# Inputs and outputs stored in memory in the order the chip uses them

## The chip, the core and the metric

The kernel runs on one core of a Trainium2 chip. The metric is the time of one execution in device microseconds (us); lower is better. Engines are TensorE (PE in the profile), VectorE (DVE), ScalarE (ACT), GpSimd (POOL) and SyncE (SP), which here issues the DMAs. Each takes its instructions in program order, and they wait for one another by semaphores.

## What is computed

One inference step of a two-layer decoder trunk on two groups that share the weights: a prompt of 512 tokens and 8 samples of 4 tokens, in float32. Layer 0 is an RWKV-7 time mixing with 32 heads of 64, layer 1 a gated MLP with causal spatial mixing in chunks of 128; each adds to a residual of width 1024, and a final RMS norm follows. What matters of layer 0:

```
def step(S, inp):                  # S: one state [value, key] per head
    r_t, w_t, k_t, v_t, kk_t, a_t = inp
    sa = einsum('bhvk,bhk->bhv', S, -kk_t)
    S = S * w_t + sa (kk_t * a_t)^T + v_t k_t^T
    return S, einsum('bhvk,bhk->bhv', S, r_t)
```

The step runs over the tokens; the prompt starts from a zero state, each sample from a state given as input (`state_wkv`, [value, key] per head). Outputs are the final states of both groups, the last projected row of each sequence (the token shift), the two groups' result rows, and the normalised v rows of the samples.

## The kernel before, in words

**Weights.** Every projection multiplies in three passes (high x high, high x low, low x high halves of float32 numbers), with 128 output features at a time. `load` (L110) brings a block of weights from memory as 8 pieces of 128 x 128, row by row out of the full matrix, on the SP queue; ScalarE makes the high half, VectorE the low half. The activations stand as [feature, token] with 272 columns per half (256 prompt tokens, 16 sample tokens).

**Start.** x is loaded with a token per partition, normalised and turned by TensorE transposes into the halves `hh` and `hl`. The parameter vectors come as rows (`r0`, `r1`, `r2`, `sst`) and are turned into columns `ng`, `prm1`, `prm2` and `ss` by transposes (L176, L225, L226, L231).

**Layer 0.** Sixteen pairs of heads p are worked on one after the other, each in many stages. Every stage is a Python generator whose `yield`s cut it into steps, and a table `AT` gives each step a due time in units (one unit is one set of three projection matmuls; a pair's four projections k, r, v, z are 64 units). `on(p, stage, ...)` puts step n of pair p at 64p + AT[stage][n], all steps are sorted by that time into `agenda`, and `play` issues them in this order. Inside `manual_schedule` this is the order of the instructions on PE, DVE, ACT, POOL and SP alike. A stage that takes 200 units is therefore spread over the periods of the next pairs. Pairs 14 and 15 have tables of their own (`smp14`, `gram15`, ...); the others share one. The stages that the steps of the prediction touch:

- `gram` (L574 on): TensorE multiplies keys with queries per chunk of 64 tokens (L584), VectorE masks the products (L587), and they go to memory and back in another layout: four stores to `du` (L592, in two steps of two at 56.2993 and 56.8544) and one load `lu` (L595, at 60.3741).
- `lanes`: inverts small triangular matrices on VectorE, beginning with `lu` times `ln` (L686, at 62.564); its result goes by `dz` through memory into `Zf` (L725, L729).
- `merge`: VectorE transposes blocks of `Zf` (L740), TensorE multiplies (L750, L751), and so on.
- `chain`: seven sequential state updates, a matmul `sb` (L890) and a VectorE update `RS` (L892) in turn; at the end TensorE transposes the final state (L900), ScalarE copies it, and it is stored.
- `sample`: four DMAs load a pair's sample states `sn` (L930) at 7.88, four transposes turn them (L934, at 64.4533), ScalarE copies them to `s0`; the steps of four tokens are solved by matrix products; VectorE adds the update to `s0` (L992) and multiplies by the decay (L994, at 119.608); four transposes turn the result back (L998, at 128.593), ScalarE copies it, and four DMAs store it (L1006) at 179.324.
- `tail` (L1061): VectorE makes the gated output `of`, stored to memory as `od` (L1063) at 179.55.
- `flip` (L799 on): in nine of the periods a block of x is loaded, turned by transposes (L813, L815) and stored to a scratch tensor `xfd`, from where the residual is loaded later.

**Layer 1** uses Tile's own order, not the table. The spatial weights are turned by transposes (L1337) and masked; u, v and z are projected; the shift outputs are turned at L1450.

## Time and profile before

| | |
|---|---|
| timed runs | 1279.21, 1276.22, 1279.21 us; median 1279.21 |
| profiled execution, first to last instruction (span) | 1272.1 us |
| runs above that span | 4.1 to 7.1 us |
| mean granted TensorE clock | 0.997 of full speed |
| moved by DMA | 124.34 MB in 271752 packets, 114673 of them under 512 B |
| share of the 16 DMA engines' time, main queue | 35.0% |

The page gives no time of the profiled execution beyond its span. In the rows, PE is TensorE multiplying, PEld its weight loads, and SPq, ACTq and so on an engine's issuing side. A row of a timeline is start, length, engine, source line, operation and tensors (out<-in), with the shapes and the count of merged instructions; a bracket at its end is idle time of the engine before it and what ended it. A row of the list of groups has the count, then the busy time in us and the mean length of one in ns. Lengths of matmuls overlap, so what one costs its engine is read from start to start.

### The profile page before, as it was taken

How to read it: one execution, taken by the hardware profiler on the slowest of the kernel's cores; microseconds unless marked ns; L12 is line 12 of the kernel's file. 1: busy time of each engine (PE TensorE's matmuls, PEld its weight loads, DVE VectorE, ACT ScalarE, POOL GpSimd, SP SyncE). 2: the span in 40 equal slices, each digit the busy share in tenths (PEclk: the TensorE clock that was granted, in tenths of full speed). 3: DMA queues.
4: the chain of work that ended last, by engine and by line, in shares of the span. 5: the costliest groups of instructions: out<-in, count | busy, mean ns of one | idle time of the engine just before them, and what ended most of it. 6: DMA issues, size and time to landing. Idle time of an engine off the chain costs nothing.

```text
span 1272.1 us, 36601 instructions
## 1 busy us (share of the span) xinstructions
PE 1244.5 (98%) x15279; PEld 1192.4 (94%) x15279; DVE 953.0 (75%) x2210; ACT 692.3 (54%) x1613; POOL 137.0 (11%) x346
## 2 busy tenths in 40 slices
PE   6999999999999999999999999999999999999997
PEld 5899999999999999999989899999999999999997
DVE  5789998989899898989988866472338656656466
ACT  5677567667766865776766562244343223223333
POOL 2212021111202111110211100110000000000000
PEclk9999999999999999999999999999999999999999
DMA  5422433432343344334333364422323232231511
GB/s 161 116 72 74 111 97 91 111 105 75 94 122 91 87 111 101 89 94 102 85 79 81 101 200 117 143 92 76 100 72 99 64 109 79 70 110 55 166 37 72
DMA packets 271752, 124.34 MB, mean 98 GB/s; under 512 B 114673, under 2 KB 264451, under 8 KB 271587
## 3 DMA queue, kind: packets, MB, share of 16 engines
q1 hardware_dynamic: 271587, 122.00, 35.0%
q8 instruction: 120, 1.97, 0.7%
q14 instruction: 45, 0.37, 0.1%
HBM read 102.02 MB, written 19.95 MB: 96 GB/s over the span
## 4 chain that ended last, share of the span: by engine, by line
PE 87%; DVE 5%; DMA 3%; ACT 2%; issue 1%; POOL 1%; SPq 1%; POOLq 0%; DVEq 0%; ACTq 0%
PE r_p L253 3%; PE v_p L253 3%; PE gz_p L253 3%; PE gu_p L253 3%; PE gz_p L255 3%; PE gz_p L254 3%; PE gu_p L255 3%; PE gu_p L254 3%; PE gv_p L1410 2%; PE k_p L253 2%; PE gv_p L1412 2%; PE gv_p L1411 2%; PE r_p L255 2%; PE r_p L254 2%; PE pgo L584 2%; PE v_p L254 2%
## 5 line engine op out<-in xcount | busy, mean ns | idle before, releaser
L253 PE MATMUL v_p<-hh,v_h 128*128 128x272 f32 x256 | 78.9, 308 | 0.9 <-ACT raw L396 0.9
L253 PE MATMUL r_p<-hh,r_h 128*128 128x272 f32 x256 | 78.5, 306 | 0.0
L253 PE MATMUL k_p<-hh,k_h 128*128 128x272 f32 x256 | 78.3, 306 | 0.0
L253 PE MATMUL z_p<-hh,z_h 128*128 128x272 f32 x256 | 77.8, 304 | 0.0
L253 PE MATMUL gz_p<-hh,gz_h 128*128 128x272 f32 x256 | 75.2, 294 | 0.0
L253 PE MATMUL gu_p<-hh,gu_h 128*128 128x272 f32 x256 | 74.2, 290 | 0.0
L255 PE MATMUL r_p<-hh,r_l 128*128 128x272 f32 x256 | 74.1, 289 | 0.0
L255 PE MATMUL gz_p<-hh,gz_l 128*128 128x272 f32 x256 | 74.0, 289 | 0.0
L255 PE MATMUL gu_p<-hh,gu_l 128*128 128x272 f32 x256 | 73.9, 289 | 0.0
L255 PE MATMUL z_p<-hh,z_l 128*128 128x272 f32 x256 | 73.8, 288 | 0.0
L255 PE MATMUL v_p<-hh,v_l 128*128 128x272 f32 x256 | 73.8, 288 | 0.0
L254 PE MATMUL gz_p<-hl,gz_h 128*128 128x272 f32 x256 | 73.8, 288 | 0.0
L254 PE MATMUL gu_p<-hl,gu_h 128*128 128x272 f32 x256 | 73.8, 288 | 0.0
L254 PE MATMUL v_p<-hl,v_h 128*128 128x272 f32 x256 | 73.7, 288 | 0.0
L254 PE MATMUL r_p<-hl,r_h 128*128 128x272 f32 x256 | 73.7, 288 | 0.0
L254 PE MATMUL z_p<-hl,z_h 128*128 128x272 f32 x256 | 73.7, 288 | 0.0
L255 PE MATMUL k_p<-hh,k_l 128*128 128x272 f32 x256 | 73.6, 288 | 0.0
L254 PE MATMUL k_p<-hl,k_h 128*128 128x272 f32 x256 | 73.6, 287 | 0.0
L1410 PE MATMUL gv_p<-gv_h,hh 128*128 128x256 f32 x256 | 73.3, 286 | 0.0
L1411 PE MATMUL gv_p<-gv_h,hl 128*128 128x256 f32 x256 | 72.1, 282 | 0.0
L1412 PE MATMUL gv_p<-gv_l,hh 128*128 128x256 f32 x256 | 72.0, 281 | 0.0
L255 PE MATMUL go__p<-goh,go_l 128*128 128x272 f32 x192 | 55.6, 289 | 0.0
(446 smaller groups left out, 4624.9 us busy)
## 6 DMA issues: line engine op xcount, KB each, us to landing
k_r<-rw_in SPq DMA_DIRECT2D x16, 512.0 KB
r_r<-rw_in SPq DMA_DIRECT2D x16, 512.0 KB
v_r<-rw_in SPq DMA_DIRECT2D x16, 512.0 KB
z_r<-rw_in SPq DMA_DIRECT2D x16, 512.0 KB
gu_r<-gm_in SPq DMA_DIRECT2D x16, 512.0 KB
gz_r<-gm_in SPq DMA_DIRECT2D x16, 512.0 KB
go_r<-gm_out SPq DMA_DIRECT2D x24, 256.0 KB
od<-of SPq DMA_DIRECT2D x16, 272.0 KB
```

Source lines behind the costliest of these rows:

```text
L253: T.matmul(ps, whi, ahi, start=first, stop=False)
L254: T.matmul(ps, whi, alo, start=False, stop=False)
L255: T.matmul(ps, wlo, ahi, start=False, stop=last)
L584: T.matmul(pg[h][:, 128 * j : 128 * j + 128], BK[rs, c].rearrange("p a b -> p (a b)"), AR[rs, :, c, :], start=True, stop=True)
L1410: T.matmul(o, ah, hi, start=k == 0 and i % 2 == 0, stop=False, skip_group_check=True)
L1411: T.matmul(o, al, hi, start=False, stop=False, skip_group_check=True)
L1412: T.matmul(o, ah, lo, start=False, stop=k == KD - 1, skip_group_check=True)
```

## The change

The host now hands over all inputs in the order in which the chip wants them and takes the outputs in the chip's order.

- Weight blocks: each partition's 8 x 128 numbers are contiguous (rows of 4 KB instead of 512 B). Sizes and engines of the loads stay.
- `ng`, `prm1`, `prm2` and `ss` are columns of the constants; 13 small loads, 11 transposes and 4 copies at the start go. The constants load is split at column 144 instead of 128 and its second part is longer.
- Sample states lie key by value: one load straight to `s0` (two buffers instead of one) and one store straight from it; 8 transposes, 2 ScalarE copies and 6 DMAs per pair go. The store's step is due at 120.608, one unit behind the decay multiply at 119.608 (pair 14: 111.185 after 110.185; pair 15: 154.2 after 153.2).
- The prompt's final state is stored as it is, in the step that also begins the y matmuls (134.984); its transpose and copy go. Before, the store was due at 189.592.
- `flip` and `xfd` go; the residual is loaded from an input `x_t`.
- The LoRA weights of a pair come by one load instead of two; the spatial weights come turned, and one multiply masks all eight; the shift output is stored as it stands.

The rest of the table `AT` is unchanged. The core of the diff:

```
         def load(name, src, nk, w=128, q=Q):
-            q.dma_start(raw[:, 0:nk, :], src.rearrange("(k p) f -> p k f", p=128))
+            q.dma_start(raw[:, 0:nk, :], src)
...
-            Q.dma_start(cst[:, 128:], A["consts"][:, 128:])
+            Q.dma_start(cst[:, 144:], A["consts"][:, 144:])
...
             py = [bank("py", t) for t in "sy"]
-            pf = bank("pfs", "g")
+            Q.dma_start(O["prompt_s"][p], SS[:, NCH, :])
...
-            T.transpose(pf[0:64, 0:128], SS[:, NCH, :], ident)
...
-            for bp in range(2):
-                for h in range(2):
-                    Q.dma_start(sn[64 * bp : 64 * bp + 64, :, 64 * h : 64 * h + 64], swk[bp, 2 * p + h])
-            yield
-            ps = bk("ps0", p)
-            for j in range(4):
-                T.transpose(ps[:, 128 * j : 128 * j + 128], sn[:, j, :], ident)
-            yield
-            s0 = l0.tile([128, 512], F32, name=f"s0{p}", tag="s0", bufs=1)
-            S.activation(s0, ps, AF.Copy)
+            s0 = l0.tile([128, 512], F32, name=f"s0{p}", tag="s0", bufs=2)
+            Q.dma_start(s0, A["state_s"][p])
...
             V.tensor_tensor(out=v8(s0), in0=v8(s0), in1=z["D"][:, 8:16, None].to_broadcast([128, 8, 64]), op=ALU.mult)
             yield
-            ps = bk("pso", p)
-            for j in range(4):
-                T.transpose(ps[:, 128 * j : 128 * j + 128], s0[:, 128 * j : 128 * j + 128], ident)
-            yield
-            so = l0.tile([128, 4, 128], F32, name=f"so{p}", tag="sn", bufs=2)
-            S.activation(so, c128(ps), AF.Copy)
-            yield
-            owk = O["sample_wkv"][0].rearrange("(j a) h v k -> a h v j k", a=2)
-            for bp in range(2):
-                for h in range(2):
-                    Q.dma_start(owk[bp, 2 * p + h], so[64 * bp : 64 * bp + 64, :, 64 * h : 64 * h + 64])
+            Q.dma_start(O["sample_s"][p], s0)
...
-            smp=(7.87945, 64.4533, 66.8469, 70.2306, ..., 115.687, 119.608, 128.593, 128.593, 179.324),
+            smp=(7.87945, 70.2306, ..., 115.687, 119.608, 120.608),
-            chain=(103.348, ..., 134.984, 135.175, 135.175, 136.551, 189.592),
+            chain=(103.348, ..., 134.984, 135.175, 135.175),
-            flip=(129.64, 132.271, 132.271, 141.972),
...
-            Q.dma_start(xT[:, m : m + 2], xfd[:, m : m + 2])
+            Q.dma_start(xT[:, m : m + 2], A["x_t"][:, m : m + 2])
...
-            for q in range(2):
-                wsr = lt.tile([128, 4, 128], F32, name=f"wsr{q}", tag="gz", bufs=3)
-                Q.dma_start(wsr, A["gm_ws"][0, 4 * q : 4 * q + 4].rearrange("g t s -> t g s"))
-                ps = wa("pws")
-                for j in range(4):
-                    T.transpose(ps[:, 128 * j : 128 * j + 128], wsr[:, j, :], ident)
+            Q.dma_start(wst, A["g_ws"])
```

## The prediction, made before the changed kernel was run

> **What bounds the kernel now.** I read the page first: engine shares, then the chain that ended last.

> ```profile
> PE 1244.5 (98%) x15279; PEld 1192.4 (94%) x15279; DVE 953.0 (75%) x2210; ACT 692.3 (54%) x1613; POOL 137.0 (11%) x346
> PE 87%; DVE 5%; DMA 3%; ACT 2%; issue 1%; POOL 1%; SPq 1%; POOLq 0%; DVEq 0%; ACTq 0%
> ```

> TensorE is busy 98% of the span and holds 87% of the chain. So each matmul that goes should bring the end nearer, as long as TensorE stays the engine that ends last. By stage (the table by stretches; its columns are PE, PEld, DVE, ACT, POOL busy with counts, granted clock, DMA share, GB/s):

> ```profile
> 300.00:400.00 100.00, 99.97 (x1512) 94.53 (x1513) 89.90 (x223) 70.15 (x181) 16.68 (x49) 1.00 0.37 96
> 950.00:1050.00 100.00, 100.00 (x859) 99.77 (x858) 68.03 (x141) 31.40 (x54) 1.43 (x2) 1.00 0.31 88
> ```

> In the gMLP stage (second row) VectorE has 32% to spare. In the RWKV stage (first row) it is at 90% beside a TensorE at 100%: two in-order queues, each feeding the other, almost equally full. What the change does to their meeting points decides, so I walked one turn of the 64-unit period (44.1 us), from the timeline of VectorE, then of TensorE:

> ```profile
> 355.98 0.24 DVE L1061 SCALAR_TENSOR_TENSOR of<-X,lnh,zs 128x32 f32<-128x32 f32 x1
> 362.53 0.68 DVE L994 TENSOR_TENSOR s<-s,D 128x512 f32<-128x512 f32 x1
> 365.05 0.41 DVE L686 TENSOR_TENSOR lu<-lu,ln 64x256 f32<-64x256 f32 x1
> 366.24 0.28 DVE L892 SCALAR_TENSOR_TENSOR RS<-sb,D,ND 128x64 f32<-128x64 f32 x1
> 395.03 0.69 DVE L587 TENSOR_TENSOR GK<-pge,cst 128x512 f32<-128x512 f32 x1 [0.61 <-PE pge L584]
> 406.64 0.68 DVE L994 TENSOR_TENSOR s<-s,D 128x512 f32<-128x512 f32 x1
> ```

> ```profile
> 365.87 0.33 PE L890 MATMUL sb<-RS,MB 128*128 128x64 f32 x2
> 366.03 0.61 PE L934 MATMUL ps<-cst,sn 128*128 128x128 f32 x4
> 366.48 0.60 PE L998 MATMUL pso<-cst,s 128*128 128x128 f32 x4
> 366.92 0.33 PE L890 MATMUL sb<-RS,MB 128*128 128x64 f32 x2
> 384.55 0.27 PE L750 MATMUL pm<-T,GK 64*64 64x64 f32 x1
> 393.82 0.37 PE L584 MATMUL pgo<-AR,BK 64*128 64x128 f32 x1
> ```

> These rows close a ring of true dependences. L994 (the sample state times its decay) ends at 363.21. VectorE reaches L686, the first operation of `lanes`, 1.84 later. L892 behind it ends 1.47 after L686 starts, and feeds the second sb matmul, 0.40 later. TensorE then runs densely to L750 (17.63) and on to the gram matmuls (9.27); VectorE masks them from 1.21 later and is dense until the next L994 ends at 407.32 (12.29). Sum 1.84 + 1.47 + 0.40 + 17.63 + 9.27 + 1.21 + 12.29 = 44.11, the period. The slack in the ring is small: about 0.25 before the sb matmul.

> The third queue is SP. Its timeline at that place:

> ```profile
> 356.25 0.34 SPq L1063 DMA_DIRECT2D od<-of  x1
> 356.64 3.77 SPq L592 DMA_DIRECT2D du<-GK  x4
> 362.10 0.59 SPq L595 DMA_DIRECT2D lu<-du  x1
> 400.75 2.57 SPq L592 DMA_DIRECT2D du<-GK  x4
> 404.90 0.59 SPq L595 DMA_DIRECT2D lu<-du  x1
> ```

> SP issues in program order and stands still at a DMA whose data are not ready: `od` goes out 0.03 after L1061 ends, and `du` only behind it. The four `du` stores and the load `lu` bring the gram products to `lanes`; L686 cannot start before `lu` lands.

> **The change, part by part.**

> *Transposes off TensorE.* Four of them take 0.45 (366.03 to 366.48) and 0.44 (366.48 to 366.92): 0.11 each from start to start, though each shows 0.27 long.

> ```profile
> L934 PE MATMUL ps<-cst,sn 128*128 128x128 f32 x64 | 9.7, 274 | 0.0
> L998 PE MATMUL pso<-cst,s 128*128 128x128 f32 x64 | 9.6, 273 | 0.0
> L813 PE MATMUL pxt<-cst,xr 128*128 128x128 f32 x32 | 4.8, 272 | 0.0
> L900 PE MATMUL pfs<-cst,RS 128*64 128x128 f32 x16 | 4.8, 298 | 0.0
> L1337 PE MATMUL pws<-cst,wsr 128*128 128x128 f32 x8 | 1.2, 275 | 0.0
> L1450 PE MATMUL psh<-cst,shl 128*128 128x128 f32 x4 | 0.7, 286 | 0.0
> ```

> These 188, with 8 small ones in the last flip and 11 at the start, at 0.11 each make 22.8 us. [...]

> *A new wait on SP.* Before, the sample state's store came after its transposes and copy, at 64p + 179.3, long after its data. Now it is at 64p + 120.608, one unit behind L994. In period p that is the store of p-1, at 64p + 56.608: between the first pair of `du` stores (56.2993) and the second (56.8544), with `lu` at 60.3741 behind. The second pair was issued around 358.5 to 360.4 while L994 ends at 363.21. So SP now stops for L994, and `du`, `lu` and L686 with it. After L994 ends: 0.03 to issue and 0.39 for the store (as `od`, 356.25 to 356.64), 1.28 for two `du` (half of 2.57), 1.58 until `lu` is issued (403.32 to 404.90), then its landing. For that:

> ```profile
> 539.15 0.59 SPq L595 DMA_DIRECT2D lu<-du  x1
> 541.73 0.41 DVE L686 TENSOR_TENSOR lu<-lu,ln 64x256 f32<-64x256 f32 x1
> 56.48 0.59 SPq L595 DMA_DIRECT2D lu<-du  x1
> 60.74 0.42 DVE L686 TENSOR_TENSOR lu<-lu,ln 64x256 f32<-64x256 f32 x1 [1.72 <-DMA lu<-du]
> ```

> In the first pair L686 found it landed 2.58 after issue; in the second it waited until 4.26. I take 2.58, the value of the steady stage. L994 to L686 becomes 0.03 + 0.39 + 1.28 + 1.58 + 2.58 = 5.86 instead of 1.84 (bounds 5.5, if `lu` lands as fast as a `du` store, 0.64 + 1.58, to 7.5).

> *The ring after.* 5.86 + 1.47 + 0.15 (an estimate of the 0.40 without its slack) + 17.08 (17.63 less four pxt, 0.44, and one pfs, 0.11) + 9.27 + 1.21 + 12.29 = 47.33: 3.22 more per period. The ps and pso transposes, the largest part removed, stood between the two sb matmuls, where TensorE now waits anyway: they give nothing there. It applies to lanes 1 to 13: with the schedules of 14 and 15, `lu` (55.849 and 39.979) is ahead of the store. 13 x 3.22 = 41.9.

> *Outside the ring.* One ps of stage 0, and ps and pso around stages 14 and 15: 6 x 0.36 = 2.2; three pfs 0.3; pws 0.9; psh 0.4; at the start 0.8. Together -4.6. The wait that opens the kernel:

> ```profile
> PE png L176 <- DMA r<-norm_g: 7.4, 1, 7.4
> PE pth L213 <- DVE xsh L204: 3.3, 1, 3.3
> ```

> png goes, but xsh, which ends that second wait, hangs on other work; no gain beyond the 0.16 of a copy.

> *The clock.* TensorE's hole before the second sb is 47.3 less some 42.9 of work: 4.4 us, in one piece, each period. What a hole does (stretches, columns as above):

> ```profile
> 19.00:21.00 2.00, 2.00 (x10) 1.61 (x10) 1.58 (x5) 2.00 (x6) 0.00 (x0) 0.52 0.18 51
> 21.00:23.00 2.00, 2.00 (x10) 1.50 (x10) 0.81 (x3) 0.63 (x2) 0.00 (x0) 0.63 0.48 134
> 1266.00:1268.00 2.00, 0.00 (x0) 0.00 (x0) 1.34 (x6) 1.57 (x4) 0.55 (x1) 1.00 0.38 158
> 1268.00:1270.00 2.00, 0.00 (x0) 0.00 (x0) 0.30 (x2) 0.28 (x1) 0.00 (x0) 0.59 0.91 375
> ```

> ```profile
> 1265.36 0.28 PE L1595 MATMUL pgl<-hh,gol 128*128 128x256 f32 x1
> ```

> After the last matmul (ends 1265.64) the clock fell at about 1268.36 (0.59 over two us): 2.7 us of idling were enough. At the start the means 0.52 and 0.63 say half clock for 96% and 74% of two stretches of 2 us, 3.4 us together, which costs 1.7 us of dense work. I take it that 8 of 10 holes cost that: 13 x 0.8 x 1.7 = 17.7 (bounds 0 and 13 x 2.5 = 32).

> *Priced at nothing.* Weight loads in rows of 4 KB: no matmul is released by one in the list of waits after the start; the next block's load is issued while the current one multiplies. Copies on ScalarE: 54% busy. The prompt-state store, now on SP ahead of the s0 and v loads, waits for the last L892; the v load slips behind it, and the plan uses that weight 11 units after its load (8.43 and 19.34). The longer constants load, the residual from memory, the one-piece mask of the spatial weights: each within 1 us either way.

> Sum: 41.9 - 4.6 + 17.7 = +55.0 on a span of 1272.1, about 1327. The runs' median lies 7.1 above the profiled span, kept: 1279.2 + 55.0 = 1334.

> **The rivals.**

> *Faster: TensorE's queue alone decides.* If SP passes the store without holding back `lu`, or VectorE has other work to absorb it, the 22.8 come off: 1256. For it: no wait over 0.3 on TensorE between 100 and 600. Against: the ring, each link of which is a queue order or data. The change turns faster where L994-to-L686 stays under 3.0 us: the period is then 0.35 longer, and 13 x 0.35 is the 4.6 saved outside the ring. 8%; the transposes' gain and a shrunken stall cancel (1279) in 4%.

> *The clock stays up.* The stall as above, but the holes don't lower the clock: 1279.2 + 41.9 - 4.6 = 1317. For it: the kernel before has no hole of this length in its middle, so no row shows one; the two falls above are at the start and at the end. 14%.

> *The clock falls only where a hole holds a whole 3.4 us stretch.* The clock at the start changed after 3.4 us; if it is set once per such a stretch, and only an entirely idle one lowers it, a hole of 4.4 us holds one in (4.4 - 3.4) / 3.4 = 3 of 10 periods: 1316.5 + 13 x 0.3 x 1.7 = 1323. Against: the fall 2.7 us after the last matmul, when no whole stretch had been idle. 12%. [...]

> *Change not effective* (the copies remain) can't be: the code that issues them is gone.

> **How the numbers follow.** Stall and clock 62% (1334), stall alone 14%, stall and some clock 12%, cancelled 4%, faster 8%. The slow cases' bounds: 13 x 0.36 = 5 under 1317 is 1312, less 5 for the edits priced at nothing, 1307; above, 13 x 1.64 = 21 over 1334 is 1355, and 1358 with a little more lost to the clock. That leaves out the faster cases (12%) and a margin of 7%. Within 0.3% (about what a measurement of this kernel can tell from no change) 0.04, faster 0.08, slower 0.88.

> **What would show it.** Right: SP waits for L994 at the new store; VectorE waits for `lu` at L686 by about 4 us, 13 times; TensorE waits for L892 at sb; period 47 to 50; stretches of granted clock below 1.00 between 100 and 650; RWKV's later stages and gMLP as before. Wrong: L686 shows no wait, the period is 43 and TensorE stays at 100%. The clock step is wrong if the clock column stays 1.00 with the holes there.

## The result, and the profile after

The changed kernel takes 1344.07 us (median of 4 runs, 1342.25 to 1348.11) against 1278.01 for the kernel before in the same session (4 runs, 1276.22 to 1279.21). The ratio is 1.0529, 95% interval 1.0511 to 1.0548: 5.3% slower. The profiled execution has a span of 1343.8 us and took 1345.54.

Three lines of the page: the engines' shares, the granted TensorE clock in 40 slices, and the shares of the chain that ended last.

```profile
PE 1252.3 (93%) x15072; PEld 1200.6 (89%) x15072; DVE 949.6 (71%) x2205; ACT 668.8 (50%) x1555; POOL 135.1 (10%) x346
...
PEclk9998999899899999999999999999999999999999
...
PE 70%; DVE 12%; DMA 9%; ACT 6%; issue 2%; SPq 1%; POOL 0%; DVEq 0%; POOLq 0%; ACTq 0%
```

TensorE issues 207 instructions fewer (15279 to 15072) and is nevertheless busy 8 us longer, because part of its work ran at a lower clock (the mean granted clock is 0.971, before 0.997): the three eights lie in the first third of the span, where the RWKV pairs are. Its share of the chain falls from 87% to 70%; DMA has gone from 3% to 9%. The list of waits, one group for each of TensorE, VectorE and SP's queue (total, times, longest):

```profile
PE sb L826 <- DVE RS L828: 61.7, 15, 5.8
DVE lu L649 <- DMA lu<-du: 58.1, 15, 5.5
...
SPq L917 <- DVE s L915: 75.5, 16, 9.0
```

In the new numbering L917 is the sample state's store, L915 the decay (before L994), L649 the first operation of `lanes` (L686), L826 and L828 the matmul `sb` and its update (L890, L892), L713, L547 and L550 the old L750, L584 and L587. The three rows are one stall at three places: SP waits for the decay, so VectorE waits for `lu`, so TensorE waits for `RS`. SP's timeline shows the order behind it:

```profile
388.50 1.31 SPq L555 DMA_DIRECT2D du<-GK  x2
395.10 0.35 SPq L917 DMA_DIRECT2D sample_s<-s  x1
395.50 2.47 SPq L555 DMA_DIRECT2D du<-GK  x2
399.65 0.59 SPq L558 DMA_DIRECT2D lu<-du  x1
```

After the first pair of `du` stores nothing is issued from 389.81 to 395.10. Then the store goes, 0.03 after the decay (below) ends at 395.07, and only behind it the second pair and `lu`. VectorE at that place:

```profile
394.39 0.68 DVE L915 TENSOR_TENSOR s<-s,D 128x512 f32<-128x512 f32 x1
402.51 0.42 DVE L649 TENSOR_TENSOR lu<-lu,ln 64x256 f32<-64x256 f32 x1 [5.53 <-DMA lu<-du]
```

From the end of the decay to L649 this period, the longest of the thirteen, takes 7.44 us; before it was 1.84.

**The account.** I took the prediction's ring apart in the same way in the 13 periods of after and of before (means; the last column is the forecast without its clock term):

| link | before | after | forecast |
|---|---|---|---|
| decay ends to first `lanes` operation | 1.88 | 6.29 | 5.86 |
| to the end of `RS` | 1.43 | 1.28 | 1.47 |
| `RS` to `pm` (L713), the wait for the `sb` matmul included | 17.92 | 19.21 | 17.23 |
| `pm` to gram, gram to mask, mask to decay | 22.9 | 22.9 | 22.77 |

From the first to the fourteenth decay the kernel after takes 645.8 us, and before 573.5. The ring's growth is 72.2; the spans differ by 71.7. All the loss is in the ring.

### The profile page after: what moved, and what is told of

Read it like the earlier page. It is cut to its first block, busy times and chain, and to the rows that moved or that the text cites. A ratio compares the mean times of both kernels' runs of the same rounds, so it can differ in the third digit from the quotient of the medians.

```text
span 1343.8 us, 35882 instructions
## 1 busy us (share of the span) xinstructions
PE 1252.3 (93%) x15072; PEld 1200.6 (89%) x15072; DVE 949.6 (71%) x2205; ACT 668.8 (50%) x1555; POOL 135.1 (10%) x346
## 2 busy tenths in 40 slices
DMA packets 113513, 119.83 MB, mean 89 GB/s; under 512 B 77992, under 2 KB 81448, under 8 KB 113352
## 4 chain that ended last, share of the span: by engine, by line
PE 70%; DVE 12%; DMA 9%; ACT 6%; issue 2%; SPq 1%; POOL 0%; DVEq 0%; POOLq 0%; ACTq 0%
DMA lu<-du 3%; PE k_p L219 3%; PE gz_p L219 3%; PE gu_p L219 2%; PE gz_p L220 2%; PE gz_p L221 2%; PE gu_p L221 2%; PE gu_p L220 2%; DMA du<-GK 2%; PE r_p L219 2%; PE k_p L220 2%; PE k_p L221 2%; PE gv_p L1312 2%; PE pgo L547 2%; PE gv_p L1313 2%; PE gv_p L1314 2%
## 5 line engine op out<-in xcount | busy, mean ns | idle before, releaser
L826 PE MATMUL sb<-RS,MB 128*128 128x64 f32 x224 | 43.1, 277 | 62.2 <-DVE RS L828 61.7
L826 PEld LDWEIGHTS sb<-RS,MB 128*128 128x128 f32 x224 | 38.4, 208 | 65.5 <-DVE RS L828 64.4
L219 PE MATMUL k_p<-hh,k_h 128*128 128x272 f32 x256 | 86.7, 339 | 0.0
L220 PE MATMUL k_p<-hl,k_h 128*128 128x272 f32 x256 | 80.9, 316 | 0.0
L221 PE MATMUL k_p<-hh,k_l 128*128 128x272 f32 x256 | 80.5, 314 | 0.0
L1313 PE MATMUL gv_p<-gv_h,hl 128*128 128x256 f32 x256 | 72.2, 282 | 0.0
```

The lines of the kernel that those rows point to most:

```text
L219: T.matmul(ps, whi, ahi, start=first, stop=False)
L220: T.matmul(ps, whi, alo, start=False, stop=False)
L221: T.matmul(ps, wlo, ahi, start=False, stop=last)
L826: T.matmul(sb[:, 0:64], MB[:, c, :], SS[:, c, :], start=True, stop=True)
L1313: T.matmul(o, al, hi, start=False, stop=False, skip_group_check=True)
```

## The experiments

Each is timed against the kernel before on the same chip (1275.9 us for e1 to e4, 1275.7 for e5 to e7, 1277.5 for e8 and e9).

**The wait alone, on the kernel before** (e3). Nothing of the change is in it but a store of `s0` at the place of the new one, into scratch memory and beside the old store:

```
             V.tensor_tensor(out=v8(s0), in0=v8(s0), in1=..., op=ALU.mult)
+            yield
+            Q.dma_start(sx[p], s0)
             yield
...
-            smp=(..., 119.608, 128.593, 128.593, 179.324),
+            smp=(..., 119.608, 120.608, 128.593, 128.593, 179.324),
```

> The kernel before, with all its transposes and old layouts, and one DMA more per pair: s0 behind the decay multiply is also stored to a scratch tensor, in a step of its own due at 120.608 (111.185 and 154.2 in pairs 14 and 15), where the changed kernel has its store. Theory: the wait alone does it. Period 6.2 + 1.3 + 0.1 + 17.6 + 9.3 + 1.2 + 12.3 = 48.0 us without the clock, a hole of about 3.9 us, the clock falls in most periods and costs 1.5 to 2.2 each: 1345 us (1330 to 1360). Rival (it is the new layout): the time of the kernel before plus the cost of 16 more stores of 256 KB, 1278 to 1284 us.

Measured 1354.46 us (1352.75 to 1358.13), ratio 1.0627 [1.0604, 1.0651]. Its waits:

```profile
DVE lu L687 <- DMA lu<-du: 56.7, 14, 6.1
PE sb L891 <- DVE RS L893: 48.6, 15, 5.6
```

One added store makes the loss, and more than the loss of the whole change; the difference, about 12 us (0.0098 of 1277), is what the other parts of the change give back, as far as the 16 added transfers themselves cost nothing. That the cause is the store's place, and not the store, the next run shows.

**The store moved behind `lu`** (e1). The change as it is, with one due time other:

```
-            smp=(..., 115.687, 119.608, 120.608),
+            smp=(..., 115.687, 119.608, 126.0),
```

> The changed kernel with one number altered: the sample state's store is due at 126.0 instead of 120.608, which puts it behind the second pair of du stores, behind lu and behind the r load on SP (pairs 14 and 15 as they were). Theory (SP stands still for L915 at this store and holds back du, lu and the first operation of lanes): the wait for lu goes, TensorE has no hole, the granted clock stays 1.00 in the RWKV stage, the period falls from about 49.7 to about 43.1 us and the time to about 1256 us (1250 to 1264). Rival (the new shapes of the loads and stores, or the prompt state's store now ahead of other loads on SP, slow the kernel): the time stays above 1300 us.

Measured 1267.16 us (1263.06 to 1269.36), ratio 0.9931 [0.9908, 0.9954]. The loss is gone and the change is a gain, but 9 us and not 22.8, and the time lies above the theory's 1264. The timelines of SP and of VectorE in one period:

```profile
358.34 0.59 SPq L558 DMA_DIRECT2D lu<-du  x1
359.03 0.60 SPq L119 DMA_DIRECT2D r_r<-w_in  x1
360.70 0.35 SPq L917 DMA_DIRECT2D sample_s<-s  x1
```

```profile
359.99 0.68 DVE L915 TENSOR_TENSOR s<-s,D 128x512 f32<-128x512 f32 x1
362.50 0.41 DVE L649 TENSOR_TENSOR lu<-lu,ln 64x256 f32<-64x256 f32 x1
```

`lu` is out 2.4 before the store, and VectorE reaches L649 1.83 after the decay, as before the change. The period is 43.43 where it was 44.11. The missing part is in the list of waits:

```profile
PE sb L826 <- DVE RS L828: 8.0, 16, 1.3
```

TensorE now reaches the second `sb` matmul about 0.5 us too early, each period (8.0 over 16 places).

**The store between `du` and `lu`** (e2), the test of the break-even point:

```
-            smp=(..., 115.687, 119.608, 120.608),
+            smp=(..., 115.687, 119.608, 120.9),
```

> The changed kernel with the sample state's store due at 120.9 instead of 120.608: behind the second pair of du stores, still ahead of lu. Theory: lu alone waits for L915, the way from L915's end to lanes shrinks from about 6.2 to about 3.1 us (0.03 + 0.39 to lu's issue, 2.7 to its landing), the period is 3.1 + 1.3 + 0.1 + 17.1 + 9.3 + 1.2 + 12.3 = 44.4 us, TensorE's hole about 1.4 us, too short for the clock; 1277 us (1270 to 1284), so about the kernel before: the point from which the change turns faster. Rival (the wait for L915 as such costs, wherever lu stands): as the changed kernel, about 1344 us. Rival (lu lands early enough anyway): as with the store far back, about 1256 us.

Measured 1295.55 us (1292.75 to 1299.43), ratio 1.016 [1.0134, 1.0185]: a miss. The way from the decay to L649 was 3.2 to 4.6 us (mean 3.7), since L649 came 2.7 to 4.1 after the issue of `lu`; and TensorE's wait, which I had put at 1.4 us and held to be too short for the clock, was some 2 us and lowered it in 5 of the 13 periods (and once more behind them, at 761); the mean granted clock is 0.989, where e1 has 0.998. The table by stretches, for two of the periods (PE, PEld, DVE, ACT, POOL busy; then granted clock, DMA share, GB/s):

```profile
232.35:235.76 3.41, 1.65 (x12) 1.34 (x11) 2.61 (x13) 0.01 (x1) 0.00 (x0) 1.00 0.37 135
235.76:239.17 3.41, 3.41 (x16) 3.41 (x17) 1.93 (x7) 1.98 (x6) 0.00 (x0) 0.50 0.00 0
276.72:280.13 3.41, 2.11 (x18) 1.97 (x16) 1.62 (x4) 0.40 (x1) 0.92 (x1) 1.00 0.85 237
280.13:283.55 3.42, 2.77 (x20) 2.56 (x21) 3.19 (x16) 1.23 (x5) 0.00 (x0) 1.00 0.06 18
```

In the first pair of rows TensorE idles for 1.76 of 3.41 us and the next stretch runs at 0.50. In the second it idles for 1.30, then for 0.65 in the next, which runs at 1.00: about the same wait, but divided between two stretches. In this run the way from `RS` to `pm` is 17.3 where the clock stayed up and 18.7 to 18.9 where it fell, so that each fall costs about 1.5. (One period has 19.0 at full clock: there TensorE waited 1.6 for VectorE ahead of `pm`.)

**The hole filled** (e4). The change as it is, with 32 unused matmuls in TensorE's hole, which hold the clock up and leave the stall:

```
+                if c == 5 and p < 13:
+                    for _ in range(32):
+                        T.matmul(sb[:, 128:400], bo, hh[:, 0, 0, :], start=True, stop=True, ...)
```

> The changed kernel, with 32 matmuls of 272 columns into unused columns of the sb bank ahead of the fifth sb matmul of pairs 0 to 12, just where TensorE waits; their results are not used. They take 32 x 0.125 = 4.0 us of a hole of about 4.7. If the rest of the loss is the clock: no stretch below 1.00 in the RWKV stage, TensorE's way from the sb matmul to the next group falls from about 19.2 to about 17.1 us, the period to about 47.5, and the time to 1344 - 13 x 2.1 = 1316 us (1308 to 1324) although 52 us of work were added. If that way is long for another reason (transfers, VectorE): no change or longer, 1340 to 1350 us.

Measured 1318.61 us (1318.02 to 1322.32), ratio 1.0344 [1.0326, 1.0363], and a mean clock of 0.999 where after had 0.971. TensorE's timeline at the hole:

```profile
336.92 0.33 PE L829 MATMUL sb<-RS,MB 128*128 128x64 f32 x2
337.05 4.27 PE L828 MATMUL sb<-hh,bo 128*128 128x272 f32 x32
341.60 0.43 PE L829 MATMUL sb<-RS,MB 128*128 128x64 f32 x2 [0.27 <-DVE RS L831]
```

`RS` still comes late (the next `sb` starts 4.68 after the last), and the median period is 47.7 us, where the forecast without a clock term said 47.33. The way from `RS` to `pm` is 17.37 (mean), where after has 19.21. The ratios differ by 0.0185, or 24 us: that is the clock's share.

**The weights alone** (e7). The kernel before, with only the weight blocks contiguous:

```
-            q.dma_start(raw[:, 0:nk, :], src.rearrange("(k p) f -> p k f", p=128))
+            q.dma_start(raw[:, 0:nk, :], src)
```

> The kernel before, with only the weights laid out in memory as the kernel after has them (contiguous rows for each partition), all else as before. The prediction priced this part of the change at nothing. Theory: no change, ratio 1.000 within 0.003 (1272 to 1280 us). Rival: larger pieces shorten the waits for weights, at the start above all: over 0.3% faster, 1265 to 1272.

Measured 1275.43 us (1273.96 to 1278.77, 12 runs), ratio 0.9998 [0.9988, 1.0009]. The page counts 156168 DMA packets instead of 271752, and the time doesn't change.

**Where the rest of the 22.8 is: TensorE's meeting points moved one after the other.** e5 is e1 with the second `sb` matmul two projection units later; e8 adds the same for the LoRA matmuls; e9 takes 0.59 of VectorE's work (`lrl`) out of the stretch from mask to decay.

```
e5  -  chain=(..., 128.258, 128.842, 128.842, 132.915, ...)
e5  +  chain=(..., 128.258, 130.1, 130.2, 132.915, ...)
e8  -  lora=(-54.2734, -17.5215, -15.1165, 2.26593, 2.48318, 2.73372, 2.73372, 9.79271, ...)
e8  +  lora=(-54.2734, -17.5215, -15.1165, 4.5, 4.6, 4.7, 4.7, 9.79271, ...)
e9  +  lora=(-54.2734, -17.5215, 2.3, 4.5, 4.6, 4.7, 4.7, 9.79271, ...)
```

> The kernel after, with the store of the sample state behind lu (as in e1), and the fifth matmul of sb two projection units later in TensorE's order. In e1 TensorE waited 8.0 us in 16 places at that matmul for RS. Theory: that wait is VectorE's part of the ring, and work put ahead of it on TensorE takes it away; 1267 less about 6 gives 1261 us, between 1257 and 1265. Rival: the ring is bound by VectorE's own chain behind the lanes, so that the wait only moves to the gram matmul: about 1267, not under 1265.

> As e6_prompt_store_behind_dz, and the first LoRA matmuls (plw, pla) two projection units later in TensorE's order. In e5 TensorE's wait had moved from sb to pla, 6.6 us in 11 places, behind the same RS on VectorE. Theory: the period of 43.40 us is that wait and 42.7 us of TensorE's work; with other work ahead of pla it goes, 13 x 0.7 = 9 off 1263: 1254 us, between 1251 and 1258. Rival: VectorE's own chain from the mask to the lanes sets the period, and the wait moves on to the next matmul that needs it (pm): 1263, not under 1260.

> As e8_lora_later, and one piece of VectorE's work (lrl, 0.59 us each period) moved from ahead of the decay to behind the RS that the fifth sb matmul needs. Theory (TensorE's queue alone decides once no wait is left): nothing more than e8, 1254, between 1250 and 1257. Rival (VectorE's chain between the mask and the lanes sets the period): 0.59 off each of 13 periods, 7 to 8 us under whatever e8 gives: 1255 where that gives 1263.

e5 took 1265.52 us, ratio 0.9913 [0.9895, 0.9931]; e8 (which has e6's store too, below) 1264.69, 0.9901 [0.9887, 0.9915]; e9 1271.43, 0.9959 [0.9942, 0.9975]. In each the theory missed. The rivals of e5 and e8 have the times, though the wait went to other matmuls than they named; e9's missed too. TensorE's idle time did not go, it moved. The largest of TensorE's waits in e5, in e8, and in e9 with VectorE's:

```profile
PE pla L419 <- DVE RS L828: 7.1, 12, 0.8
```

```profile
PE pbk L609 <- ACT xw L424: 9.5, 13, 0.7
```

```profile
DVE MB L813 <- PE pm L795: 10.6, 14, 1.4
...
PE pbk L609 <- ACT xw L424: 9.5, 13, 0.7
```

The period is 43.40 in e5 (where nothing disturbs it), 43.53 in e8 and 43.95 in e9. In e9 the way from mask to decay is 12.29 as ever: with less of its own work there, VectorE waits for TensorE's `pm` at L813 instead, and `lrl` costs 0.42 where it was put. So neither queue alone sets the period. At least three meeting points (`RS` for `pla`, `xw` for `pbk`, `pm` for `MB`) lie within some 0.7 us of the limit. Each of the three is seen as the wait of one order; an order that would bring the whole 22.8 was not found.

**The prompt state's store later** (e6). e5, with this store behind the load of `dz`:

```
             py = [bank("py", t) for t in "sy"]
-            Q.dma_start(O["prompt_s"][p], SS[:, NCH, :])
...
                 yield
+            Q.dma_start(O["prompt_s"][p], SS[:, NCH, :])
...
-            chain=(..., 134.984, 135.175, 135.175),
+            chain=(..., 134.984, 135.175, 135.175, 143.0),
```

> As e5_sb_moved, and the store of the prompt state behind the load of dz, not ahead of the loads of s0 and v. The prediction priced the early place of this store at nothing. Theory: the loads behind it have time to spare, so the time is within 3 us of e5_sb_moved (1258 to 1264 where that gives 1261). Rival: the store waits on SP for its data and holds back the loads of s0 and v, so that taking it away gives over 4 us.

Measured 1262.86 us (1261.37 to 1265.78), ratio 0.9897 [0.988, 0.9914]. That is 2.7 under e5, inside the theory's bound, with overlapping intervals; the 13 periods together differ by 0.7 (566.3 and 566.9 us). The price of nothing stands within this. It has the lowest median of all the kernels timed: 1.0% under the kernel before, with the changed data layout and two stores and one matmul in other places.

## Why the prediction was right, step by step

**The stall: right.** The prediction put the store "between the first pair of `du` stores and the second", so that "SP now stops for L994, and `du`, `lu` and L686 with it". SP's timeline shows it and e3 makes it alone. One period of after has the terms almost as worked out (0.03 + 0.34 for the store, 0.05 between, 1.25 for `du`, 1.60 to the issue of `lu`, 2.62 to its landing: 5.89, where I had 5.86). The mean is 6.29, because `lu` mostly landed a little later (up to 2.9 after its issue), in the worst period the second `du` pair took 2.47 instead of 1.28, and in another `lu` was issued 2.60 behind that pair instead of 1.58. In the ring that is 4.41 more instead of 4.02, 5.1 us over 13 periods.

**The clock: right in kind, 6 us too small.** I gave it 13 x 0.8 x 1.7 = 17.7. It fell to 0.50 in all 13 periods (first at 102.22 us, last at 699.55), and the way from `RS` to `pm`, 19.21, is 1.86 above the 17.35 of e1's typical period, which has the same matmuls at full clock: 13 x 1.86 = 24. e4 gives the same 24 by another way. That refutes the rival "the clock stays up" (1317). It also refutes the rival of the whole idle stretch (1323), and e2 shows where that one fails. In after the clock changed only at the borders of stretches of 3.41 us, as that rival had it, but in e2 1.76 us of idling in one of them was enough. The four stretches of after that hold one hole:

```profile
146.57:149.98 3.41, 2.77 (x23) 2.63 (x22) 1.61 (x3) 0.40 (x1) 1.50 (x3) 1.00 0.37 115
149.98:153.40 3.42, 0.00 (x0) 0.00 (x0) 0.97 (x5) 0.00 (x0) 0.00 (x0) 1.00 0.71 150
153.40:156.81 3.41, 3.21 (x14) 3.22 (x15) 3.24 (x14) 0.57 (x3) 0.00 (x0) 0.50 0.06 25
156.81:160.23 3.42, 3.42 (x41) 3.10 (x41) 2.17 (x5) 2.43 (x6) 0.00 (x0) 1.00 0.02 5
```

The stretch that was idle throughout is followed by one at 0.50, and this, busy for 3.21 of its 3.41 us, by one at 1.00. Here the hole covered a whole stretch and ended with it; where it ran on into the next by 0.41 us or more, the half clock lasted for two (6.83 us, in 8 of the 13).

**Outside the ring: wrong.** Of the -4.6 only 0.6 came. (The sum takes four transposes there at 0.36; its own rows show 0.44, by which its 2.2 would be 2.6.) Up to the first decay after is 2.0 us faster than before, but after, e1, e2 and e4, which begin alike, take 97.0, 99.2, 94.5 and 95.6 to that point, so that these 2.0 are no more than what executions differ by. At the start the two waits of 7.4 and 3.3 were replaced by one of 11.1, for the same `xsh`. From the fourteenth decay to the first matmul of layer 1 after takes 174.8 us and before 172.2. e1 has 175.0, e6 174.1 and e8 172.9. Up to 1.7 of these 2.6 us are one more stretch at half clock (812.19 to 815.61, granted 0.50): e4, whose instructions from here on are those of after, runs at 1.00 throughout and takes 172.1. What else makes them stays open.

**The sum.** The forecast added 55.0 to the span, the run 71.7. The ring without the clock gave 6.2 of the difference (the stall 5.1, smaller links the rest), the clock 6.5, the part outside 4.0. The median came out only 10 higher than forecast since it lies 0.3 above the profiled span here, and not 7.1 as in the runs shown with the kernel before; that this made the miss smaller is luck.

**The rival on the other side was mis-priced.** It gave 1256 "if SP passes the store without holding back `lu`". e1 is that case and takes 1267. The step that fails is "the 22.8 come off": it values a transpose at its 0.11 in TensorE's queue. But the same prediction had said that the transposes between the two `sb` matmuls give nothing where TensorE waits, and the ring as written down (1.84 + 1.47 + 0.06 + 17.29 + 9.28 + 1.21 + 12.29, e1's rows) is shorter only by 0.34 in the wait ahead of the second `sb` (0.40 to 0.06) and 0.34 in TensorE's dense part (17.63 to 17.29). What goes beyond that slack, TensorE waits out. The break-even of 3.0 us counted the 4.6 that hardly came; without them e1's links give 44.11 - 41.41 = 2.7, and e2's 3.7 lies above both.

**Priced at nothing: right where tested.** The weights (e7) within 0.12%, the prompt state's store (e6) within 3 us.

## What to carry to other kernels

When a store comes to stand right behind its data in an in-order issue queue, look at what is queued behind it: here the store itself took 0.34 us to issue, and the load behind it, which a whole ring of engines was waiting for, came 4.4 us later a period. Price removed work by the link of the ring in which it lies and not by its engine's share of the span: up to 1.4 us less of TensorE's work a period gave 0.7, because three meeting points were almost tied. And price a stall on TensorE by more than its own length: here the clock fell to 0.50 at each of 13 holes, and the dense work behind each took 1.86 us longer, 24 us in all.

## What the runs showed of the hardware that was not expected

Of the 271752 DMA packets the change leaves 113513, and most of that is worth nothing in time here: e7 takes away 115584 of them by the weights alone, at a ratio of 0.9998.
